# The last layer's modulation products move from the last block's attention into the recurrence, 24 of their steps behind its first inverse

## The chip, the cores and the metric

One core of one Trainium2 chip. The metric is the device time of one execution in microseconds (us), median of several runs. Profiles come from one profiled execution each; times inside it count from the start of its span. "Granted clock" is the share of full speed that TensorE's clock had; it has two levels, 1.2 GHz (0.50) and 2.4 GHz (1.00), and a stretch's figure is their mean.

## The reference, cut to what matters

Two stacked networks of two layers each act on 256 tokens of width 1024 (float32). Every layer is modulated: a condition vector, through SiLU, times a 1024 x 6144 matrix gives six rows (shift, scale, gate, twice).

```python
for l in range(2):                       # second network
    mod = (silu(c) @ ada_w[l] + ada_b[l])
    sh1, sc1, g1, sh2, sc2, g2 = split(mod, 6)
    h = rms_norm_2(x, norm1_g[l]) * (1 + sc1) + sh1
    y = even_mixer_2(h) if l % 2 == 0 else odd_mixer_2(h)   # attention
    x = x + g1 * y
    h = rms_norm_2(x, norm2_g[l]) * (1 + sc2) + sh2
    x = x + g2 * hier_moe(h)
```

The first network's second layer has a gated recurrence instead of attention. `wkv_scan` walks the tokens with S <- S*w - (S kk)(kk a)^T + v k^T in two directions, first over 256 context tokens, then over the 256 tokens of x, for 16 heads. The modulations depend on the condition vectors alone, so they can be computed at any time before they are used.

## The kernel before, in words

**Recurrence (`odd1`, L686).** The scan is computed in chunks of 64 tokens. The 16 heads are taken as two groups of eight, each first over the context, then over x: four passes, g = 0 to 3. A pass has four parts. `rw_feat` (L970) makes the features of a head pair (four calls per pass, each for two directions: small matmuls at L989, L1046 and L1056, many DVE and ACT operations, stores of `kb`, `ar` and `rb` to DRAM on ACT's DMA queue). `rw_inv` (L1085) inverts triangular blocks on DVE by 31 pairs of operations (L1101, L1102), each needing the one before. `rw_post` (L1105; `rw_post2` for g = 3) completes the inverses with 32x32 matmuls. `rw_chain` (L1165) takes the four chunks in order: a product with the inverse (L1220), state updates and output products (L172). Features of later passes are called inside earlier chains by `ahead(p)` and the table `pos`.

**Side work.** `ada_unit` (L191) is a generator for one 512-column piece of a modulation: a 1024 x 512 weight block against the condition, eight matmuls at L203 into one PSUM bank, of which four can run beside each other on four column groups of the array. The profile counts two MATMUL instructions for each, so 16 for a unit. Then come one ACT copy (L209), eight instructions at L213 (column form) or two at L217 (row form), and small DVE sinks (L255 or L271 and L273); a row unit also loads its bias and stores its result on GpSimd's queue (L264, L268, L275). The generator yields after each two matmuls: a step, of four MATMUL instructions. A unit has four steps. `tick(n, i)` (L227) draws n steps and ties each drawn matmul behind matmul i in TensorE's order, through `anchor`. `ada2(l)` (L1408) is all of the second network's layer l: 12 units, 48 steps.

In the recurrence a step loads its own 512 KB (`wn` = 2) on SP's queue into one of two buffers (`weights(2)`); the PSUM pool of the units has one buffer (`phase((3, 2, 1), 0)`). In the last block a step shares a 1 MB load with the next (`wn` = 4), out of ten buffers, and the PSUM pool has two buffers.

**Who draws.** `layer1` (L1288) sets the recurrence's side work: `gates(1, 0)`, `mods(1, 1)`, `gates(1, 1)`, `ada2(0)`, 80 steps. The table `tk` (L1284) says how many are drawn: one or two behind a feature matmul (four per head pair), and four behind each chunk's product at L1220, two for g = 2. The places offer 120; the 80 run out with the features that pass 1 calls for pass 2. `layerB(0)` (L1992) sets `ada2(1)`; its 48 steps are drawn in `causal_scores` (L1455): 24 in `even2` (L1489, layer 0's attention), 24 in `odd2` (L1562, layer 1's).

**Order.** The tile framework fixes each engine's order at build time, with program order as the priority and a timeline of its own for when operands are ready. On the chip each engine and each DMA queue goes through its list in that order. After the recurrence the two side buffers' place goes to the two tiles of x, reloaded on GpSimd's queue at L887 and needed by the residual at L385.

Of the kernel before, what the change touches and what calls it, by code (L numbers as in the profile page):

```python
# [110 lines left out]
class K:  # L111
# [55 lines left out]
    def chain(self):  # L167

        prev = [None]

        def mm(*a, **k):
            i = self.nc.tensor.matmul(*a, **k)  # L172
            if prev[0] is not None:
                self.after(i, prev[0])
            prev[0] = i
            return i
        return mm
# [486 lines left out]
class L1(K):  # L664
# [21 lines left out]
    def odd1(self, xs, cst, Acol, Bcol):  # L686
# [131 lines left out]
        with self.phase((3, 2, 1), 0) as ph:  # L818
            self.pl = ph.es.enter_context(tc.tile_pool(name="pl", bufs=1, space=PSUM, reuse_waits="tile"))
            gp = ph.pool("gp")  # L820
            St = [self.T(gp, [P, 2, 4, P], f"St{c}") for c in range(2)]
            E3 = [self.T(gp, [P, 4, 65], f"E3{d}") for d in range(2)]
            for c in range(2):
                nc.gpsimd.memset(St[c], 0.0)
                nc.gpsimd.memset(E3[c][:, :, 64 * c:64 * c + 1], 1.0)
            E = dict(E3=E3, kT=kTd, kkn=kknd, rT=rTd, St=St, twl=twl, tal=tal, hpar=hpar, hka=hka, vd=vd,
                     ms=mstrict, mi=mincl, rmask=rmask, yd=yd, Y1=Y1, bon=bon, rkI=rkI, kbd=[self.tc.dram_tile([2, 4, P, 4, P], F32, name=f"kb_dram{g}") for g in range(4)],
                     ard=[self.tc.dram_tile([2, 4, P, 4, P], F32, name=f"ar_dram{g}") for g in range(2)],
                     rbd=[self.tc.dram_tile([2, 4, P, 8, 64], F32, name=f"rb_dram{g}") for g in range(2)])
            st = None  # L830
            self.nq = 4
            F = self.rw_open(0, False, gp)
            for hp in range(4):
                self.rw_feat(hp, gp, E, F)
            for g in range(4):
                N = {"hp": 0}

                def ahead(p):

                    while g < 3 and N["hp"] < 4 and self.pos[g][N["hp"]] <= p:  # L840
                        if N["hp"] == 0:
                            N["F"] = self.rw_open((g + 1) // 2, g % 2 == 0, gp)
                        self.rw_feat(N["hp"], gp, E, N["F"])
                        N["hp"] += 1
                ahead(0)
                self.rw_inv(gp, F)
                ahead(1)
                rest = (self.rw_post2 if g >= self.g2 else self.rw_post)(gp, F)
                st = self.rw_chain(gp, E, F, st, ahead, rest)
                ahead(9)  # L850
                F = N.get("F")
                if F:
                    Fl = F
            F = Fl

            self.do(self.side)
            E.update(z=z, J=J, sgl=sgl, behind=F["inv"])
            sl = slice(512, 1024)
            nc.gpsimd.dma_start(lng1, A["lng"][sl].partition_broadcast(P))
            nc.gpsimd.dma_start(g21, A["g2"][:, sl])  # L860
            t2 = lambda n: self.T(gp, [P, 512], n, bufs=3 if n in ("BK", "ARx") else 2)
            lng, lnb, g2 = (t2("BK") for _ in range(3))
            nc.gpsimd.dma_start(lng, A["lng"][0:512].partition_broadcast(P))
            nc.gpsimd.dma_start(lnb, A["lnb"][0:512].partition_broadcast(P))
            nc.gpsimd.dma_start(g2, A["g2"][:, 0:512])
            for t in range(2):
                rows = slice(t * P, (t + 1) * P)
                y, y1 = t2("KB"), t2("ARx")
                nc.scalar.dma_start(z[:, t, :], vd[0][rows, 0:512])
                nc.scalar.dma_start(y, yd[0][rows, :])  # L870
                nc.scalar.dma_start(y1, yd[1][rows, :])
                self.rw_bonus(0, t, E, z[:, t, :], lnb)
                self.rw_readout(t, E, y, y1, t2("RB"), lng, g2, z[:, t, :])
            lnb = t2("BK")
            nc.gpsimd.dma_start(lnb, A["lnb"][sl].partition_broadcast(P))
            for t in range(2):
                nc.scalar.dma_start(z1[:, t, :], vd[0][t * P:(t + 1) * P, sl])
                self.rw_bonus(1, t, E, z1[:, t, :], lnb)
# [402 lines left out]
    def q(self, n):  # L1281
        return getattr(self.nc, self.qs[n])

    tk = ((1, 0), (1, 0), (1, 0), (1, 0)), ((1, 2), (1, 2), (1, 2), (1, 2)), (4, 4, 2, 4)  # L1284
    late, g2 = 1, 3
    pos = ((3, 4, 9, 9), (9, 9, 9, 9), (4, 9, 9, 9), (5, 9, 9, 9))

    def layer1(self):  # L1288
        nc = self.nc
        xs, cst = self.xs[:2], self.xs[2:]  # L1290
        self.at, self.side = "unit", chain(self.gates(1, 0), self.mods(1, 1), self.gates(1, 1), self.ada2(0))
        self.odd1(xs, cst, *self.modc[1, 0])
        self.early2()
        with self.phase() as ph:
            self.ar = ph.pool("ar1")
            self.ws = ph.pool("ws3", 2)
            self.mlp(xs, 1, *self.modc[1, 1], [0, 0], 1)
# [94 lines left out]
class B2(L1):  # L1392
# [600 lines left out]
    def layerB(self, l):  # L1993
        nc, A = self.nc, self.A
        xs = self.xs[:2]
        with self.phase() as ph:
            self.ar = ph.pool(f"arB{l}")
            self.ws = ph.pool(f"wsB{l}", 2)
            Ac, Bc = self.bmods[l]
            if l == 0:  # L2000
                self.at, self.side = "unit", self.ada2(1)
            hT = self.norm_mod_T(xs, Ac, Bc, [0, 0], rs=self.rn)
            mix = (self.even2 if l == 0 else self.odd2)(hT, ph)
            if l:
                self.do(self.side)
            else:
                self.flush()
            G = self.T(self.ar, [P, D], "gates", bufs=1)
            self.row(G, f"bda{l}", 2, 0)
            logits = self.out2(mix, A["b_out"] if l == 0 else A["n_out"], xs, G, *self.router(l))  # L2010
        with self.phase(ns2=5) as ph:
            self.ar = ph.pool(f"arM{l}")
            hs = [self.T(self.ar, [P, 2, D], n, F32R) for n in ("mo_hh", "mo_hl")]
            xd = [self.T(self.ar, [P, KT, 256], "mo_xd", bufs=2) for _ in range(1)]
            hb = [self.T(self.ar, [P, D], f"mo_h{t}") for t in range(2)]
            rows = []
            for b in (4, 3, 5):
                rows.append(self.T(self.ar, [P, D], f"mo_row{b}"))
                self.row(rows[-1], f"bda{l}", b, 0)
            if l:  # L2020
                fg = self.T(self.ar, [P, D], "mo_fin")
                nc.gpsimd.dma_start(fg, A["fin_g"].partition_broadcast(P))
                self.fin = fg, hb
            self.rn = self.moe(xs, l, logits, rows, hb, *hs)
            if l:
                for t in range(2):
                    if t:
                        nc.vector.tensor_scalar(hb[t], hb[t], self.rn[t], None, ALU.mult)
                    else:
                        nc.scalar.activation(hb[t], hb[t], AF.Copy, scale=self.rn[t])  # L2030
                    nc.sync.dma_start(self.out[t * P:(t + 1) * P, :], hb[t])
# [54 lines left out]
```

## Time and profile before

| | us |
|---|---|
| median of 3 runs (lowest, highest) | 2259.72 (2257.11, 2260.31) |
| profiled execution, its own time | 2250.88 |
| its span, first to last instruction | 2248.9 |
| mean granted clock | 0.936 |
| PE, DVE, ACT, POOL busy in the span | 2075.3, 1159.6, 856.6, 119.8 |

How to read it: a busy PE is not PE at its peak, since matmuls are pipelined and a slow clock makes them longer. What a piece of work costs is read from the stage in which it runs: which engine is full there, and which wait ends last. The recurrence stands at about 800 to 1291 us, its output projection until about 1330, the MLP until about 1500, layer 0's attention of the last network at about 1600 to 1670, layer 1's at about 1950 to 2060.

### The profile page before, as it was taken

The page shows a single profiled execution, that of the slowest core. Times are in us where ns is not written, and L with a number is a line of the kernel's source. Part 1 is how long each engine was busy: PE and PEld are TensorE (multiplying, and loading weights), DVE is VectorE, ACT ScalarE, POOL GpSimd, SP SyncE. Part 2 cuts the span into 40 slices and gives each one's busy share as a digit, 9 for nine tenths or more (in the row PEclk, how much of TensorE's full clock was granted, in tenths as well). Part 3 has the DMA queues.
Part 4 walks back from the last instruction along what each step waited for, and adds up shares of the span by engine and source line. Part 5 has one row for each costly group of instructions (what it writes and reads, how often), then busy time and mean ns, then how long its engine had stood idle before and what let it go on. Part 6 is the DMA issues. An engine that isn't in the chain of part 4 may idle for free. (4 is left out here: it accounts for less than half of the span.)

```text
span 2248.9 us, 32827 instructions
## 1 busy us (share of the span) xinstructions
PE 2075.3 (92%) x13114; PEld 1451.2 (65%) x13114; DVE 1159.6 (52%) x2419; ACT 856.6 (38%) x1650; POOL 119.8 (5%) x216
## 2 busy tenths in 40 slices
PE   7999899999989989899997789998998989999897
PEld 4864688888866675685652569987765439646542
DVE  2247543433465536866826265666664236475433
ACT  3334443322352446564432345544452114243211
POOL 0100000000021000001111100000000000010000
PEclk9999999999999998759897889999998999999898
DMA  7448212222332426736886555537464959452494
GB/s 285 142 186 322 76 73 94 94 94 94 113 128 89 140 100 211 228 92 200 263 280 192 177 217 183 187 118 272 171 252 163 386 202 354 156 206 96 179 383 173
DMA packets 124310, 414.53 MB, mean 184 GB/s; under 512 B 20608, under 2 KB 59152, under 8 KB 88432
## 3 DMA queue, kind: packets, MB, share of 16 engines
q1 hardware_dynamic: 59824, 340.03, 41.1%
q10 hardware_dynamic: 55552, 50.95, 7.3%
q0 software_dynamic: 8768, 21.31, 3.1%
q8 instruction: 107, 1.75, 0.3%
q14 instruction: 59, 0.48, 0.1%
HBM read 383.30 MB, written 28.93 MB: 183 GB/s over the span
## 5 line engine op out<-in xcount | busy, mean ns | idle before, releaser
L164 DVE TENSOR_TENSOR wlo<-wraw,whi 128x1024 fp32r<-128x1024 f32 x252 | 308.0, 1225 | 405.6 <-ACT whi L161 398.3
L161 ACT ACTIVATE whi<-wraw 128x1024 fp32r<-128x1024 f32 x252 | 265.4, 1058 | 490.2 <-PE mm L189 234.6
L187 PE MATMUL mm<-hT_h,whi 128*128 128x256 f32 (+1 forms) x832 | 268.2, 333 | 2.3 <-ACT whi L161 2.3
L188 PE MATMUL mm<-hT_l,whi 128*128 128x256 f32 (+1 forms) x832 | 267.3, 328 | 0.0
L189 PE MATMUL mm<-hT_h,wlo 128*128 128x256 f32 (+1 forms) x832 | 242.2, 327 | 0.5 <-DVE wlo L164 0.3
L203 PE MATMUL ada<-wraw,csil 128*32 128x512 f32 x768 | 148.1, 663 | 30.7 <-DMA wraw<-in_bda 19.7
L187 PEld LDWEIGHTS mm<-hT_h,whi 128*128 128x128 f32 x832 | 157.4, 191 | 19.8 <-ACT whi L161 4.0
L188 PEld LDWEIGHTS mm<-hT_l,whi 128*128 128x128 f32 x832 | 158.6, 191 | 14.9
L189 PEld LDWEIGHTS mm<-hT_h,wlo 128*128 128x128 f32 x832 | 149.2, 190 | 16.3 <-DVE wlo L164 1.5
L188 PE MATMUL mm<-wlo,b 128*128 128x512 f32 x384 | 151.3, 394 | 0.1
L189 PE MATMUL mm<-whi,b 128*128 128x512 f32 x384 | 150.8, 393 | 0.0
L1934 PE MATMUL ada<-wraw,mo_xd 128*64 128x512 f32 x512 | 135.5, 599 | 0.0
L187 PE MATMUL mm<-whi,b 128*128 128x512 f32 x384 | 135.1, 393 | 0.0
L310 PE MATMUL tr<-s,x 128*128 128x128 f32 x288 | 57.0, 342 | 50.4 <-DVE s L301 20.0
L188 PE MATMUL mm<-wlo,hT_h 128*128 128x512 f32 (+1 forms) x256 | 98.8, 388 | 1.4 <-DVE wlo L164 1.4
L189 PE MATMUL mm<-whi,hT_l 128*128 128x512 f32 (+1 forms) x256 | 95.9, 388 | 0.0
L187 PE MATMUL mm<-whi,hT_h 128*128 128x512 f32 (+1 forms) x256 | 95.3, 398 | 0.5 <-ACT whi L161 0.4
L310 PEld LDWEIGHTS tr<-s,x 128*128 128x128 f32 x288 | 48.9, 240 | 62.0 <-issue 33.7
L188 PEld LDWEIGHTS mm<-wlo,b 128*128 128x128 f32 x384 | 72.0, 188 | 17.9 <-DVE wlo L164 0.8
L187 PEld LDWEIGHTS mm<-whi,b 128*128 128x128 f32 x384 | 72.0, 188 | 16.6
L189 PEld LDWEIGHTS mm<-whi,b 128*128 128x128 f32 x384 | 72.0, 188 | 16.4
L1934 PEld LDWEIGHTS ada<-wraw,mo_xd 128*64 128x64 f32 x512 | 38.1, 136 | 67.9 <-issue 67.7
(520 smaller groups left out, 3714.6 us busy)
## 6 DMA issues: line engine op xcount, KB each, us to landing
wraw<-in_w SPq DMA_DIRECT2D x64, 1024.0 KB, 4.8
wraw<-in_moe_gu SPq DMA_DIRECT2D x64, 1024.0 KB, 7.8
wraw<-in_ada SPq DMA_DIRECT2D x32, 1024.0 KB, 7.2
wraw<-in_moe_d SPq DMA_DIRECT2D x32, 1024.0 KB, 7.1
wraw<-in_bda SPq DMA_DIRECT2D x48, 512.0 KB, 4.7
wraw<-in_bda SPq DMA_DIRECT2D x24, 1024.0 KB, 4.8
wraw<-in_ada SPq DMA_DIRECT2D x32, 512.0 KB, 4.8
wraw<-in_b_in SPq DMA_DIRECT2D x12, 1024.0 KB, 11.5
```

What stands on the lines that cost most here:

```text
L161: nc.scalar.activation(h, src, AF.Copy)
L164: nc.vector.tensor_tensor(l, src, h.bitcast(F32), ALU.subtract)
L187: mm(ps, ah, bh, start=first, stop=False)
L188: mm(ps, ah, bl, start=False, stop=False)
L189: mm(ps, al, bh, start=False, stop=last)
L203: i = nc.tensor.matmul(ps[q:q + 32, :], lhs[:, k, :], raw[:, j % self.wn, :], start=k < nq, stop=k >= 8 - nq, tile_position=(0, q))
L310: nc.tensor.matmul(pt[:, j, :], xs[e + j][:, k * P:(k + 1) * P], dall[:, e + j, :], start=True, stop=True)
L1934: nc.tensor.matmul(pg[64 * e:64 * e + 64, :], xd[:, k, s0:s0 + 64], gu[e](k), start=k == 0, stop=k == KT - 1, tile_position=(0, 64 * e))
```

## The change

After `rw_inv` of pass g, `ti[g]` steps are drawn without an anchor: 24 for g = 0, none for the others. Pass 2 draws four steps per chunk instead of two. `ada2(1)` is appended to the recurrence's side work, 128 steps in all, and `layerB` no longer sets or drains any; the calls of `tick` in `even2` and `odd2` stay, and draw nothing.

```diff
                 ahead(0)
                 self.rw_inv(gp, F)
+                self.tick(self.ti[g])
                 ahead(1)
...
-    tk = ((1, 0), (1, 0), (1, 0), (1, 0)), ((1, 2), (1, 2), (1, 2), (1, 2)), (4, 4, 2, 4)
+    tk = ((1, 0), (1, 0), (1, 0), (1, 0)), ((1, 2), (1, 2), (1, 2), (1, 2)), (4, 4, 4, 4)
+    ti = (24, 0, 0, 0)
...
-        self.at, self.side = "unit", chain(self.gates(1, 0), self.mods(1, 1), self.gates(1, 1), self.ada2(0))
+        self.at, self.side = "unit", chain(self.gates(1, 0), self.mods(1, 1), self.gates(1, 1), self.ada2(0), self.ada2(1))
...
-            if l == 0:
-                self.at, self.side = "unit", self.ada2(1)
             hT = self.norm_mod_T(xs, Ac, Bc, [0, 0], rs=self.rn)
             mix = (self.even2 if l == 0 else self.odd2)(hT, ph)
-            if l:
-                self.do(self.side)
-            else:
-                self.flush()
```

## Rows read from the trace of the kernel before

**Rows 1.** Stages in windows: busy us (instructions) of each engine, granted clock, DMA share.

```profile
core 0: us, PE busy (x) PEld busy (x) DVE busy (x) ACT busy (x) POOL busy (x), PEclk, DMA share, GB/s
917.00:1016.00 99.00, 93.47 (x638) 75.96 (x640) 77.26 (x215) 61.67 (x149) 1.11 (x2) 0.59 0.45 131
1016.00:1180.00 164.00, 151.03 (x2175) 94.33 (x2173) 93.70 (x234) 68.77 (x124) 22.72 (x43) 0.94 0.81 253
1180.00:1257.00 77.00, 58.58 (x744) 25.80 (x744) 48.57 (x104) 20.99 (x35) 10.86 (x21) 0.80 0.63 197
1257.00:1291.00 34.00, 24.32 (x440) 19.55 (x438) 4.23 (x9) 11.94 (x20) 3.18 (x7) 0.91 0.46 146
1291.00:1332.00 41.00, 30.29 (x113) 22.57 (x114) 30.34 (x46) 19.96 (x34) 0.00 (x0) 0.91 0.75 305
1603.00:1669.00 66.00, 63.64 (x402) 36.02 (x400) 42.17 (x151) 33.47 (x105) 2.60 (x5) 1.00 0.67 251
1960.00:2028.00 68.00, 64.56 (x391) 27.70 (x383) 51.38 (x188) 27.55 (x103) 7.89 (x14) 0.93 0.55 203
```

**Rows 2.** The same windows, line L203 alone: PE busy (x), PEld busy (x), clock, DMA.

```profile
845.00:917.00 72.00, 14.62 (x64) 2.00 (x64) 0.87 0.76 233
917.00:1016.00 99.00, 0.00 (x0) 0.00 (x0) 0.59 0.45 131
1016.00:1180.00 164.00, 45.41 (x176) 6.13 (x176) 0.94 0.81 253
1180.00:1257.00 77.00, 22.86 (x80) 2.83 (x80) 0.80 0.63 197
1603.00:1669.00 66.00, 13.83 (x96) 2.66 (x96) 1.00 0.67 251
1960.00:2028.00 68.00, 13.75 (x96) 2.72 (x88) 0.93 0.55 203
```

**Rows 3.** The same windows, lines L213 (first row) and L217 (the others) alone.

```profile
1603.00:1669.00 66.00, 4.21 (x32) 3.87 (x32) 1.00 0.67 251
1603.00:1669.00 66.00, 2.04 (x4) 0.17 (x4) 1.00 0.67 251
1960.00:2028.00 68.00, 6.24 (x12) 0.52 (x12) 0.93 0.55 203
```

**Rows 4.** PE's groups at L203: in 1016 to 1180, then in 1180 to 1257 (last column: idle before).

```profile
L203 PE MATMUL ada<-wraw,csil 128*32 128x512 f32 x176 | 45.4, 657 | 11.7 <-DMA wraw<-in_bda 3.6 <-DMA wraw<-in_ada 3.6 <-DVE bB L255 2.4
L203 PE MATMUL ada<-wraw,csil 128*32 128x512 f32 x80 | 22.9, 777 | 17.0 <-DMA wraw<-in_bda 16.1 <-DVE adb L271 1.0
```

**Rows 5.** PE and DVE in time order: start, us, what [idle before and releaser].

```profile
1187.14 1.05 PE L203 MATMUL ada<-wraw,csil 128*32 128x512 f32 x4 [3.45 <-DMA wraw<-in_bda]
...
1193.85 1.06 PE L203 MATMUL ada<-wraw,csil 128*32 128x512 f32 x8
...
1254.27 1.92 PE L203 MATMUL ada<-wraw,csil 128*32 128x512 f32 x4 [0.68 <-DMA wraw<-in_bda]
...
1328.33 1.27 DVE L385 SCALAR_TENSOR_TENSOR x<-yo,ss,x 128x1024 f32<-128x1024 f32 x1
```

**Rows 6.** GpSimd's queue in time order, and two DMA issues of 1180 to 1257.

```profile
1256.50 1.06 POOL L887 DMA_DIRECT2D x<-x_dram  x2 [9.24 <-DMA UV<-v_dram]
...
wraw<-in_bda SPq DMA_DIRECT2D x18, 512.0 KB, 4.5
...
x<-x_dram POOLq DMA_DIRECT2D x1, 512.0 KB, 5.8
```

**Rows 7.** Waits of 907 to 985; even2's attention as a window; DVE's L271 in 1960 to 2028.

```profile
DVE AB L1074 <- PE tr L1056: 6.4, 5, 1.6
DVE AB L1069 <- PE tr L1056: 3.2, 4, 1.6
...
1618.00:1653.00 35.00, 35.00 (x246) 18.97 (x245) 27.55 (x115) 18.33 (x64) 0.00 (x0) 1.00 0.64 243
...
L271 DVE TENSOR_TENSOR adb<-ada,adb 2x512 f32<-2x512 f32 x6 | 4.0, 675 | 1.1 <-PE ada L217 1.1
```

## The prediction

> **What bounds the kernel now.** I read the stages as windows first, then the same windows for L203 alone, then the orders of PE and of GpSimd's queue at the ends of stages. The side work has three surroundings. In 917 to 1016, the first inverses, there is none of it: L203 counts zero, PE is busy 93.5 of 99 us, but at a granted clock of 0.59, with DVE at 77.3 [rows 1, 2]. From 1016 to 1256 it runs without a break, at a pace of its own: 176 instructions, four to a step, make 44 steps in 164 us, 3.73 us each, then 20 steps in 77 us, 3.85 each [rows 2]. The anchors aren't the limit: the last steps drawn hang on pass 2's features and run in the middle of pass 3's chain. The limit is the load of 512 KB through two buffers. It lands in 4.5 us [rows 6]; in 1180 to 1257 PE stood idle 16.1 us before L203 for it, in the 164 us before only 7.2 [rows 4]. From 1257 to 1291 there is no side work. In the last block the 48 steps sit in stages in which PE is full: 63.6 of 66 us in layer 0's attention, 64.6 of 68 in layer 1's [rows 1], with no wait for weights there.
>
> So the change takes PE time out of two full stages, puts half of it beside a cold stretch, and hangs the other half onto a queue that is already late. The sign is decided by when the last side step ends.
>
> **What is moved.** 48 steps are 192 instructions at L203, 12 copies at L209, 32 instructions at L213 (four units), 16 at L217 (eight), the sinks on DVE; on SP 24 loads of 1 MB go and 48 of 512 KB come; on GpSimd's queue ten loads and eight stores of rows move to the recurrence.
>
> **Last block, gain.** Side work there takes 13.8 + 4.2 + 2.0 = 20.0 us of PE in the first window and 13.8 + 6.2 = 20.0 in the second [rows 2, 3]. Instructions overlap a little in these sums, so 37 us is the upper bound. What is late next is DVE: it keeps 42.2 us in the first, less two L271 at 0.675, so 40.8, and 51.4 - 4.0 = 47.4 in the second [rows 1, 7]. It doesn't fill a stage of softmaxes that wait in turn for PE and ACT: its share in the attention part was 27.55 of 35.00, 0.79 [rows 7]. At that share the stages take 40.8 / 0.787 = 52 and 47.4 / 0.787 = 60 us, 14 and 8 less. I take **-22**; the lower bound is -8, if only the less crowded half of it comes back. The 24 loads that leave SP's queue there give nothing: PE's groups in these windows show no wait for weights.
>
> **The 24 steps behind the first inverses.** Without an anchor, and ahead of almost everything else by program order, they can run as their loads land: at 3.73 us a step 24 take 90 us, within the 99 that are empty of side work. They are two units of columns left of `mods(1, 1)`, `gates(1, 1)`, and two of `ada2(0)`. PE: 24 x 45.41 / 44 = 24.8 us, and six units' ends, four at 4.21 / 4 and two at 2.04 / 2, 6.2; together 31 [rows 2, 3]. If PE stays at 0.59 there is no room: 31 us measured near 0.94 become 49, and 93.5 + 49 = 143 against 99, a loss of 44. If the clock is what it was in 1016 to 1180 with side work, 0.94, the old work shrinks to 93.5 x 0.59 / 0.94 = 59; with 31, and 7.2 / 44 = 0.16 us of waiting per step, that is 94 us. The best that can come is DVE's 77, so -22. I take 0.94, since 1016 to 1180 is the nearest stretch that mixes small matmuls with these steps: **-5** for the start of pass 0's chain. Behind a waiting L203 stand L1056 and L989 of the features and L1122 of `rw_post` on PE, and DVE waits for these already (9.6 us at L1069 and L1074 [rows 7]); that is why a gain above 5 isn't taken.
>
> The rule of the Trainium skill on this (TensorE: Matmul & The Clock Gate, section "What's actually happening") is that the throttled clock is the default and activity releases it. By a full release the old work would take 93.5 x 0.59 = 55 us, with 35 of new 90, and the term would be -9 in place of -5.
>
> **The 24 steps at the end.** The other 24 are drawn in pass 2 and come last in the queue. Up to there order and lag are as before, with the gained 5 us: the side work stands at about 1256.2 - 5 = 1251 (the last step starts at 1254.27 and takes 1.92 [rows 5]) with 24 steps to go. For the pace I take the end of the old work, 18 steps with starts from 1193.85 to 1254.27, so 60.4 / 17 = 3.55 us [rows 5]: 24 x 3.55 = 85, and the last step ends at 1336. The lower bound is two loads in flight and nothing else in the way, (4.5 + 1.05) / 2 = 2.8 us, end at 1318; the upper bound is above 3.85, for loads that share the DMA engines with the output projection's weights (DMA share 0.75 in 1291 to 1332 [rows 1]).
>
> Who waits for that: pass 3's chain, whose products queue behind waiting steps (as 3.45 us at 1187 did [rows 5]); PE has 34 - 24.3 and 41 - 30.3, so 20 us, idle from 1257 to 1332 for 24.8 + 8 x 1.02 = 33 us of new PE work, which takes some 13 us more than there is. Later than that is x: its two tiles lie where the side buffers lay, and its loads were issued at 1256.50, right at the end of the last step, after 9.24 us of waiting [rows 6]. The profile names a DMA as releaser; the time fits the step. They land 5.8 us later. At 1336 this gives 1342, and L385, which needs x, stood at 1328.33 [rows 5]. So the recurrence ends **+14** later, the 5 us already in it; the 13 of PE work lie beside that. KB loads of the chain and the rows' small transfers share GpSimd's queue; I cost them at nothing beside the 14, and at up to 10 where x's loads are laid ahead of a chain's load.
>
> **Sum.** -22 + 14 = -8 us: the profiled execution's 2250.9 becomes 2243. The median is 8.8 us above that execution, and the same difference on it gives 2252.
>
> **Rivals.**
>
> (a) *The side work outlasts the projection; slower.* With -22 in the last block the point at which it decides is an end of the last step at 1336 + 8 = 1344, a pace of 93 / 24 = 3.9 us. That is hardly above the 3.85 of 1180 to 1257, and the new loads also meet four loads of 1 MB for the projection, on the same SP queue. At 4.4 us the end is 1251 + 106 = 1357, x comes at 1363, 35 late, and the sum is +13: 2273. For it: the 16.1 us of waits [rows 4]. Against it: after 1291 neither chain nor features compete. Chance 0.26.
>
> The Trainium skill (DMA: Bandwidth & Descriptors, section "Queues, rings and completion order") says that a DMA engine takes turns between the queues it has work for, packet by packet. By that rule the side loads and the projection's slow each other, and it speaks for (a); no row here shows the two together.
>
> (b) *The attention cools; no change.* Without the dense steps PE may not keep 1.00 there. The first inverses show small matmuls alone at 0.59 [rows 1]. At 0.70 layer 0's stage needs (63.6 - 20) / 0.70 = 62 us on PE, 4 less than now, and layer 1's (64.6 - 20) x 0.93 / 0.70 = 59, 9 less: -13 + 14 = +1, 2261. Against it: projections run beside both stages. Chance 0.18.
>
> (c) *The cold stretch stays cold*, or the 24 steps aren't laid there: +44 in place of -5, 2301. Against it: 0.94 and 0.87 wherever features and L203 ran together [rows 2]. Chance 0.06.
>
> (d) *Both ends good*: pace 2.8, so that x isn't late, and -30 in the last block: some 2230. Chance 0.08.
>
> **How the numbers follow.** The forecast has 0.42. A measurement of this kernel tells 0.2%, 4.5 us, from no change. Faster by more: forecast and (d), 0.50; within: (b), 0.18; slower: (a) and (c), 0.32. The range leaves out (c), half of (d) and the far end of (a): 2229 to 2284. The forecast's own spread, with the pace from 3.4 to 3.85 and the last block from -17 to -30, is 2240 to 2264.
>
> **What would show it.** Right: about 96 instructions of L203 between 917 and 1016 and a granted clock near 0.9 there; pass 0's first product at L1220 some 5 us earlier; L203 until about 1336; x loaded right behind its last step and L385 some 14 us late; the two attention stages at about 52 and 60 us, still at 0.9 or more. Wrong: L385 more than 22 us late, attention stages that shrink by less than 14 us together, or a first stretch longer than 99 us.

## The result and the profile after

The change makes the kernel slower: 2332.77 us median of four runs (2325.98 to 2337.05) against 2259.94 (2257.11 to 2260.31), a ratio of 1.0322 (95% interval 1.0295 to 1.0349). The forecast was 2252 with a range of 2229 to 2284; the result lies outside. The profiled execution of the changed kernel took 2325.98 us, its span is 2324.2 us, its mean granted clock 0.920. Medians are taken over undisturbed executions; one of e7's four, 2411.82 us at a clock of 0.891, is left out as slow.

Cutting both traces at the same instructions shows where the 75 us of span went (us; starts of the instructions named):

| from, to | before | after | difference |
|---|---|---|---|
| span's start, first inverse | 907.8 | 903.4 | -4.4 |
| first inverse, last chain product (L1220, now L1221) | 378.0 | 377.6 | -0.4 |
| last chain product, residual L385 | 42.5 | 120.8 | +78.3 |
| L385, first scores of layer 0's attention | 275.4 | 275.3 | -0.1 |
| first to last scores there | 48.1 | 35.2 | -12.9 |
| last scores, first scores of layer 1's attention | 295.6 | 296.8 | +1.2 |
| first scores there, first product of its MoE | 154.7 | 170.0 | +15.3 |
| first product of its MoE, end | 146.6 | 145.1 | -1.5 |

One place carries the loss, the 121 us behind the last chain product. The two attention stages, which were to give back 22 us, give back nothing together.

The stages as windows of the changed kernel (line numbers are one or two higher from L847 on), in the order of [rows 1]: busy us (instructions) of PE, PEld, DVE, ACT, POOL, granted clock, DMA share, GB/s. Then layer 0's attention (1677 to 1712) and layer 1's.

```profile
917.00:1016.00 99.00, 89.31 (x704) 56.94 (x705) 69.00 (x190) 56.17 (x133) 4.14 (x8) 0.83 0.75 234
1016.00:1180.00 164.00, 147.18 (x2083) 87.22 (x2078) 111.65 (x281) 72.42 (x136) 25.83 (x48) 0.94 0.81 256
1180.00:1257.00 77.00, 66.22 (x988) 39.39 (x984) 37.53 (x76) 25.03 (x42) 6.46 (x12) 0.85 0.60 192
1291.00:1332.00 41.00, 16.48 (x36) 1.66 (x36) 6.66 (x7) 5.20 (x6) 2.50 (x5) 0.52 0.89 353
...
1677.00:1692.00 15.00, 14.42 (x85) 10.01 (x83) 11.18 (x32) 10.64 (x25) 0.00 (x0) 1.00 0.47 151
1692.00:1712.00 20.00, 19.41 (x107) 10.80 (x107) 17.27 (x82) 10.61 (x45) 0.00 (x0) 1.00 0.11 45
...
2027.00:2047.00 20.00, 19.31 (x71) 9.94 (x73) 13.00 (x49) 5.95 (x26) 0.00 (x0) 0.50 0.00 0
2047.00:2067.00 20.00, 20.00 (x76) 9.53 (x73) 9.86 (x37) 5.26 (x23) 0.00 (x0) 0.50 0.01 1
2067.00:2096.00 29.00, 25.90 (x108) 12.12 (x108) 15.38 (x58) 7.97 (x34) 0.00 (x0) 0.62 0.00 1
```

Three things are to be seen. In 1291 to 1332, where the output projection ran before with 113 matmuls, PE now has 36, DVE 7 instructions, and DMA is at 0.89. Layer 0's attention is shorter at a full clock. In layer 1's, PE is busy nearly without a break and yet at 0.50, and DMA does nothing.

Line L203 alone in 917 to 1016, 1016 to 1180, 1180 to 1257 and behind the last chain product (PE, PEld, clock, DMA, GB/s); [rows 2] answer to it:

```profile
917.00:1016.00 99.00, 24.47 (x93) 3.15 (x92) 0.83 0.75 234
1016.00:1180.00 164.00, 42.81 (x168) 5.86 (x168) 0.94 0.81 256
1180.00:1257.00 77.00, 19.84 (x84) 2.52 (x80) 0.85 0.60 192
1281.00:1364.00 83.00, 30.43 (x80) 3.64 (x80) 0.59 0.71 258
```

The first stretch took its 24 steps (93 instructions). But 80 instructions, 20 steps, still stand behind the last chain product, in 83 us. PE in order of time there:

```profile
1281.03 1.15 PE L1221 MATMUL mm<-rhs,AB 64*64 64x64 f32 x32 [0.43 <-ACT rhs L1215]
...
1300.81 3.43 PE L203 MATMUL ada<-wraw,csil 128*32 128x512 f32 x8 [4.92 <-DMA wraw<-in_bda]
1318.53 3.19 PE L203 MATMUL ada<-wraw,csil 128*32 128x512 f32 x8 [14.29 <-DMA wraw<-in_bda]
...
1359.28 1.74 PE L203 MATMUL ada<-wraw,csil 128*32 128x512 f32 x4 [0.58 <-DMA wraw<-in_bda]
1361.78 1.02 PE L217 MATMUL ada<-adp,sel 128*2 128x512 f32 x2 [0.76 <-ACT adp L209]
1362.73 0.66 PE L899 MATMUL tr<-ident,z 128*128 128x128 f32 x4
...
1364.07 0.50 PE L187 MATMUL mm<-whi,moh 128*128 128x512 f32 x1
```

From 1287 to 1362 PE has nothing but side steps, most of them after a wait for their load; L899, which prepares the projection's operand, follows without a gap behind the last, and the projection's first product 1.3 us later. So the projection waits for no data of its own: it stands in PE's list behind the steps (e5 tests it). The load of x on GpSimd's queue and the residual, which ends the stage:

```profile
1361.33 1.06 POOL L888 DMA_DIRECT2D x<-x_dram  x2 [7.56 <-PE ada L203]
...
1401.86 1.27 DVE L385 SCALAR_TENSOR_TENSOR x<-yo,ss,x 128x1024 f32<-128x1024 f32 x1
```

The longest wait, 14.3 us, is explained by SP's queue, and by its loads of 1286 to 1320 (KB each, median us from issue to landing):

```profile
1286.06 1.61 SPq L151 DMA_DIRECT2D wraw<-in_wo  x3
1287.97 5.73 SPq L151 DMA_DIRECT2D wraw<-in_bda  x2
1293.74 0.42 SPq L151 DMA_DIRECT2D wraw<-in_wo  x1
1294.46 5.32 SPq L151 DMA_DIRECT2D wraw<-in_w  x5
1302.76 1.84 SPq L151 DMA_DIRECT2D wraw<-in_bda  x2
```

```profile
wraw<-in_w SPq DMA_DIRECT2D x6, 1024.0 KB, 15.8
wraw<-in_wo SPq DMA_DIRECT2D x4, 1024.0 KB, 10.5
wraw<-in_bda SPq DMA_DIRECT2D x4, 512.0 KB, 14.1
```

`in_w` are the MLP's weights. Five blocks of 1 MB that nobody needs before the projection is done were issued just ahead of two side loads of 512 KB. The four side loads issued in this stretch, two behind the projection's blocks (`in_wo`) and two behind the MLP's, landed after 14.1 us (median) in place of 4.5 [rows 6].

### The profile page after: what moved, and what is told of

It is laid out like the page before. It is cut to its first block, busy times and chain, and to the rows that moved or that the text cites. A ratio compares the mean times of both kernels' runs of the same rounds, so it can differ in the third digit from the quotient of the medians.

```text
span 2324.2 us, 32897 instructions
## 1 busy us (share of the span) xinstructions
PE 2106.3 (91%) x13114; PEld 1442.3 (62%) x13114; DVE 1161.5 (50%) x2419; ACT 857.6 (37%) x1650; POOL 119.8 (5%) x216
## 5 line engine op out<-in xcount | busy, mean ns | idle before, releaser
L164 DVE TENSOR_TENSOR wlo<-wraw,whi 128x1024 fp32r<-128x1024 f32 x252 | 307.5, 1223 | 419.6 <-ACT whi L161 412.9
L161 ACT ACTIVATE whi<-wraw 128x1024 fp32r<-128x1024 f32 x252 | 266.0, 1060 | 509.8 <-PE mm L189 237.6
L203 PE MATMUL ada<-wraw,csil 128*32 128x512 f32 x768 | 175.8, 687 | 64.2 <-DMA wraw<-in_bda 52.3
L203 PEld LDWEIGHTS ada<-wraw,csil 128*32 128x32 f32 x768 | 25.3, 114 | 124.8 <-DMA wraw<-in_bda 72.7
L209 ACT ACTIVATE adp<-ada 128x512 f32<-128x512 f32 x48 | 28.5, 594 | 151.2 <-PE ada L203 148.7
L187 PEld LDWEIGHTS mm<-whi,b 128*128 128x128 f32 x384 | 72.0, 188 | 16.6
```

Of the source, the lines that this page charges most:

```text
L161: nc.scalar.activation(h, src, AF.Copy)
L164: nc.vector.tensor_tensor(l, src, h.bitcast(F32), ALU.subtract)
L187: mm(ps, ah, bh, start=first, stop=False)
L203: i = nc.tensor.matmul(ps[q:q + 32, :], lhs[:, k, :], raw[:, j % self.wn, :], start=k < nq, stop=k >= 8 - nq, tile_position=(0, q))
L209: nc.scalar.activation(part[kr], ps[kr], AF.Copy)
```

## The experiments

Theory: the last side steps lag behind their places, the loads set their pace, and the projection stands behind all of them in PE's list; layer 0's attention gains, layer 1's loses its clock. The rivals stand with each run. `ada2a(l)` yields the first 24 steps of `ada2(l)` (the columns and row 2), `ada2b(l)` the other 24 (rows 3, 4, 5). Medians in us, each beside runs of the kernel before on the same chip; that kernel's median differs by up to 10 us between chips, so totals from different chips are compared as differences from it. The ratio is estimated from the runs of both and isn't the quotient of the two medians:

| kernel | median | before | ratio (95%) |
|---|---|---|---|
| changed kernel | 2332.77 | 2259.94 | 1.0322 (1.0295 to 1.0349) |
| e1_cold_only | 2233.78 | 2258.14 | 0.9889 (0.9847 to 0.9931) |
| e2_half | 2240.72 | 2258.14 | 0.9914 (0.9886 to 0.9941) |
| e3_warm | 2306.12 | 2258.14 | 1.0196 (1.0141 to 1.0252) |
| e5_behind | 2271.63 | 2257.88 | 1.0048 (1.0017 to 1.0079) |
| e6_four_buffers | 2316.37 | 2257.88 | 1.0243 (1.0168 to 1.0318) |
| e7_no_cold | 2384.82 | 2257.88 | 1.0538 (1.0455 to 1.0620) |
| e8_router | 2234.38 | 2257.88 | 0.9900 (0.9840 to 0.9960) |
| e9_56_steps | 2213.76 | 2249.62 | 0.9827 (0.9796 to 0.9858) |
| e10_24_behind | 2220.99 | 2249.62 | 0.9892 (0.9834 to 0.9950) |
| e11_odd_late | 2297.07 | 2249.62 | 1.0201 (1.0161 to 1.0242) |
| e12_48_behind | 2248.69 | 2257.08 | 0.9966 (0.9941 to 0.9991) |

Lengths of stages in each trace (us). A trace is one execution, and its own time lies between 17 us below its kernel's median (e5) and 10 above it (e9). A first inverse to pass 0's first product at L1221; B to the last chain product; C to L385; D from there to the MLP's residual; E first to last scores of layer 0; F first scores of layer 1 to its MoE.

| kernel | A | B | C | D | E | F |
|---|---|---|---|---|---|---|
| before | 92.1 | 285.9 | 42.5 | 192.7 | 48.1 | 154.7 |
| changed kernel | 91.2 | 286.5 | 120.8 | 192.7 | 35.2 | 170.0 |
| e1 | 94.0 | 262.2 | 44.0 | 192.7 | 48.1 | 155.9 |
| e2 | 90.2 | 283.0 | 42.4 | 191.9 | 35.2 | 157.0 |
| e3 | 93.4 | 282.0 | 120.3 | 192.7 | 35.2 | 152.4 |
| e4 | 88.5 | 278.8 | 79.3 | 192.7 | 35.2 | 149.7 |
| e5 | 89.0 | 274.0 | 46.3 | 204.1 | 35.2 | 170.3 |
| e6 | 87.5 | 282.2 | 105.9 | 192.0 | 47.4 | 155.6 |
| e7 | 93.4 | 296.2 | 166.4 | 192.7 | 35.2 | 171.6 |
| e8 | 88.7 | 262.2 | 42.6 | 192.4 | 42.4 | 155.4 |
| e9 | 88.3 | 251.5 | 43.6 | 200.0 | 48.1 | 153.1 |
| e10 | 87.5 | 262.3 | 42.6 | 198.3 | 35.2 | 154.0 |
| e11 | 93.4 | 282.6 | 43.4 | 192.7 | 48.1 | 205.4 |
| e12 | 88.1 | 244.9 | 46.3 | 238.3 | 35.2 | 156.5 |

**One part alone: the 24 unanchored steps.**

```diff
 (the kernel before)
+                self.tick(self.ti[g])        # behind rw_inv
+    ti = (24, 0, 0, 0)
```

> The kernel before with 24 of its 80 recurrence steps drawn behind the first inverses; the last layer's 48 steps stay in the last block. Theory: the only effect is the first product of pass 0, 5 us earlier, since the same stretch of the changed kernel gained 5 us: about 2255 us (2250 to 2259), no change in the last block. Rival: the 80 steps now run out some 90 us earlier, near 1170, and what comes after them in passes 2 and 3 is cooler than the granted clock of 0.80 that 1180 to 1257 had, or shows no gain: 2260 to 2275.

2233.78 us, 24 less, outside both ranges. Column A did not shrink (94.0), but B did, by 24 us: the side work runs out at 1189, and passes 2 and 3 go on without it. The clock is near what [rows 1] had there, 0.81 in 1180 to 1270. So the steps that the kernel before ran in passes 2 and 3 were in the chain's way, at about 1 us a step, and what the 24 places behind the inverses bring is that fewer stand there. On which engine or queue they were in the way isn't separated.

**Half of the move.** On top of e1:

```diff
-        ... self.gates(1, 1), self.ada2(0))
+        ... self.gates(1, 1), self.ada2(0), self.ada2a(1))
-            if l == 0:                       # layerB
-                self.at, self.side = "unit", self.ada2(1)
+            if l:
+                self.at, self.side = "unit", self.ada2b(1)
```

> 104 steps in the recurrence (24 behind the first inverses, the first 24 of the last layer at the end of the queue, pass 2 at two per chunk as before), the other 24 steps in layer 1's attention as before, none in layer 0's. Theory: the 104th step started at 1270 in the changed kernel, before its last chain product, so the projection isn't held up: -5 at the first inverses, -13 in layer 0's attention, layer 1's attention at a granted clock of 1.00 as before: about 2242 us (2234 to 2250). Rival: the end of the recurrence is held up by these 24 steps too, by 10 to 20 us: 2252 to 2262.

2240.72: the theory holds. C is 42.4, as before: 104 steps end in time. E is 35.2, F 157.0. The 5 us that the theory put at the first inverses came as 1.9 in A and 2.9 in B, so there it was right by its sum only. Against e1 the 24 steps in passes 2 and 3 cost B 21 us and bring E 13.

**Matmuls put back into layer 1's attention.** The changed kernel (cut; called behind the scores, 8 times, with n = 3, so 48 matmuls, which the profile counts as 96):

```diff
+        for k in range(2 * n):
+            q = 32 * (k % 4)
+            i = self.nc.tensor.matmul(ps[q:q + 32, :], self.cs2[:, k % KT, :], ...
```

> The changed kernel with matmuls of the same size as the 24 side steps put back into layer 1's attention, on operands that already lie in SBUF, into a bank that nobody reads: no load, no copy, no sink. Theory (clock): the granted clock of that stage, 0.50 to 0.62 for 80 us, comes back to 0.9 or more, and the stage is as long as it was in the kernel before: 2333 - 16 = 2317 us (2312 to 2323), although PE has some 16 us more to do. Rival (it was the loads, or the order of the work, and not the matmuls): the matmuls only add, 2333 to 2350, with a clock below 0.7.

F fell to 152.4 with more work in it, and the clock is back:

```profile
2036.00:2056.00 20.00, 18.72 (x114) 8.58 (x114) 14.30 (x56) 7.61 (x33) 0.00 (x0) 1.00 0.00 1
2056.00:2076.00 20.00, 19.77 (x127) 8.50 (x129) 12.94 (x50) 6.00 (x26) 0.00 (x0) 1.00 0.01 1
2076.00:2101.00 25.00, 22.95 (x135) 11.11 (x131) 15.95 (x60) 8.68 (x38) 0.00 (x0) 0.93 0.00 1
```

DMA is as idle as in the changed kernel, so it is the matmuls, not their loads. Each against its own before, the total gained 25 us (72.8 to 48.0), F in the two traces 17.6. The median lies 6 us below the theory's range; where these came from isn't shown.

**The same from the other side.** The kernel before, without the draws in `odd2`:

```diff
-        self.tick(steps, i)
+        if steps < 3:
+            self.tick(steps, i)
```

> The kernel before, with the 24 steps of layer 1's attention drawn behind that attention and not in it. Theory (these steps keep the clock of that stage): the granted clock falls to 0.5 to 0.65 between the first scores and the output projection, the stage from the first scores to the MoE's first product grows from 155 to 170 us or more, and the total to 2258 + 15 = 2273 us, and up to 15 more where the 24 steps aren't hidden by the output projection (2270 to 2290). Rival (they only fill PE, and the attention is shorter without them): 2245 to 2262, with a clock above 0.8.

2297.07, 47 above its own before where the theory had 12 to 32, so beyond its range on its side: F is 205.4. The attention ran at 0.50 from 1965 to 2060, and the 24 steps came on top:

```profile
1965.00:1985.00 20.00, 19.03 (x67) 9.82 (x65) 14.51 (x57) 6.75 (x30) 0.00 (x0) 0.50 0.00 0
1985.00:2005.00 20.00, 18.60 (x71) 9.04 (x71) 8.39 (x31) 4.69 (x19) 0.00 (x0) 0.50 0.00 1
```

**Last steps without loads.** The changed kernel (cut); rows 3 to 5 of the last layer are computed from a tile that lies in SBUF:

```diff
-                if j % self.wn == 0:
+                if self.res is None and j % self.wn == 0:
...
-  raw[:, j % self.wn, :]
+  raw[:, j % self.wn, :] if self.res is None else self.res
```

> The changed kernel, whose last 24 side steps read a tile that already lies in SBUF in place of their weight blocks, so that 12 MB of loads in the recurrence are left out and three rows of the last layer's modulation are not what they should be; every matmul, copy, sink and small transfer stays. Theory (the loads set the pace of the last steps, and the output projection stands behind them on PE): the last step ends before 1290 and the residual's first half stands near 1325 to 1335 in place of 1402: about 2262 us (2255 to 2275). Rival (the units' own chain through one PSUM bank, or the work on PE, holds them up): the last step ends after 1330, 2300 us or more.

The total says nothing here: the wrong rows feed the router, and layer 1's MoE ran its first products with 1024 matmuls in place of 256. In the recurrence the last step started at 1313.9, 46 us earlier, and L385 at 1357.3, 44.6 earlier. So loads are the larger part of the lateness, and the projection moves with the last step; but the theory's 1290 was missed (the last step ended at 1315, short of the rival's 1330). What held the steps up next, in PE's order:

```profile
1287.44 1.02 PE L217 MATMUL ada<-adp,sel 128*2 128x512 f32 x2 [0.78 <-ACT adp L209]
1303.18 3.34 PE L203 MATMUL ada<-rwc,csil 128*32 128x512 f32 x16 [14.73 <-DVE adb L271]
```

and on ACT and DVE:

```profile
1299.09 2.00 ACT L161 ACTIVATE whi<-wraw 128x1024 fp32r<-128x1024 f32 x2 [9.82 <-DMA wraw<-in_w]
...
1300.18 2.36 DVE L164 TENSOR_TENSOR wlo<-wraw,whi 128x1024 fp32r<-128x1024 f32 x2 [9.46 <-ACT whi L161]
1302.46 0.67 DVE L271 TENSOR_TENSOR adb<-ada,adb 2x512 f32<-2x512 f32 x1
```

The row's sink L271 stands in DVE's list behind a split of the weights (L161 and L164), which waits for one of the MLP's blocks of 1 MB. The units have one PSUM bank, and the next step waits for the sink.

**Last steps behind the projection.** The changed kernel:

```diff
-        ... self.ada2(0), self.ada2(1))
+        ... self.ada2(0), self.ada2a(1))
                     half(j, u, ps[u][j])
+            self.do(self.ada2b(1))
```

> The changed kernel, whose last 24 side steps (three rows of the last layer) are drawn behind the recurrence's output projection in program order, not ahead of its end. Theory (the projection stands behind these steps in PE's order): the residual's first half comes some 80 us earlier than 1402, near 1325; the 24 steps then take their 25 us of PE, and 6 for their units' ends, ahead of or inside the MLP, which has no PE to spare: 2333 - 78 + 30 = 2285 us (2275 to 2296). Rival (the loads are the cost wherever they stand): 2310 us or more.

2271.63, 3 us below the theory's range: C is 46.3, so the 24 steps had held the projection up for 75 us. Behind it they cost D 11 us for 31 of PE work, less than the theory took; here they share loads of 1 MB in eight buffers, and wait for none of them. PE of this kernel:

```profile
1269.93 1.15 PE L1222 MATMUL mm<-rhs,AB 64*64 64x64 f32 x32 [0.75 <-ACT rhs L1216]
...
1276.02 2.07 PE L940 MATMUL tr<-y,rwc 128*128 128x512 f32 x2 [2.49 <-DVE mol L903]
...
1279.92 1.03 PE L187 MATMUL mm<-whi,moh 128*128 128x512 f32 x2
```

The projection starts 10 us after the last chain product (L1222 in this kernel), against 83.

**Fewer early loads.** The changed kernel with `self.weights(4)` in place of `self.weights(8)` behind the recurrence.

> The changed kernel with four weight buffers of 1 MB in place of eight behind the recurrence, so that the projection's four loads fill them and the MLP's six early loads of 1 MB can't share the DMA engines with the last side steps (they had held the first step after 1301 up by 14 us). Theory (contention): the last side step starts near 1346 in place of 1360, the residual near 1388, and the total gains what the MLP doesn't lose by its later loads: 2318 to 2333 us. Rival (the steps are as late without these loads): last step at 1355 or later, total 2330 to 2345.

The last step started at 1344.3 and L385 at 1386.6, as the theory said; C is 15 us shorter, D stayed at 192.0, and the total is 14 us less, each against its own before (2316.37 is 2 below the theory's range). PE's idle time before L203 behind the last chain product, in 1281 to 1364, fell from 33.6 to 24.8 us for `in_bda` (changed kernel, then this one):

```profile
L203 PE MATMUL ada<-wraw,csil 128*32 128x512 f32 x80 | 30.4, 974 | 35.9 <-DMA wraw<-in_bda 33.6 <-DVE adb L271 2.3
L203 PE MATMUL ada<-wraw,csil 128*32 128x512 f32 x80 | 27.1, 812 | 27.4 <-DMA wraw<-in_bda 24.8 <-DVE adb L271 2.4
```

So the MLP's early loads cost some 15 us. This run also shows layer 0's attention long and layer 1's short, with no steps in either; see the end.

**The cold places undone.** The changed kernel with `ti = (0, 0, 0, 0)`.

> The changed kernel without the 24 steps behind the first inverses: all 128 steps are tied to matmuls, the last of them in pass 3's chain. Theory (the 24 steps behind the first inverses cost nothing there, and each step at the end costs about 3.5 us, since loads set the pace and the projection stands behind them): 24 x 3.5 = 84 us more: 2333 + 84 = 2417 us (2395 to 2430). Rival (the loads behind the inverses only put off other traffic, and the side work catches up before the end): 2330 to 2360.

2384.82: 54 more than the changed kernel, each against its own before, where 84 were expected. In the trace B grew by 10, C by 46: the last step starts at 1421.9, 62 us later, so a step at the end costs 2.6 us, not 3.5. The side work catches up a little, by its pace once nothing else runs: 38 steps in 127 us are 3.3 each. The value lies between theory and rival, nearer to the theory.

**Places of a lower price.** e8 moves 16 steps behind layer 0's router logits (e1 with this and the matching order of units, cut):

```diff
+            if l == 0:                       # moe, behind logits(i)
+                self.do(self.side)
```

> 80 steps in the recurrence, 24 of them behind the first inverses; of the last layer's 48 steps 8 stay in layer 0's attention, 16 move behind that layer's router logits, where PE was idle for 6 of 22 us at a granted clock of 0.69, and 24 stay in layer 1's attention. Theory (a step costs by the room that its stage has): layer 0's attention gives back 16 x 0.54 = 9 us, the router takes some of it: 2234 - 5 = 2229 us (2220 to 2236). Rival (the steps stand ahead of the router's own small matmuls on PE, which nothing hides): 2240 to 2255.

2234.38, in the upper part of the theory's range, and no gain on e1. E gave back 5.7, not 9, and the way from the last scores to the MoE's first product took it: 61 us in e1, 73 here. The rival's mechanism holds, at a smaller price than it named.

e9 and e10 move 24 steps each behind the projection, e12 both:

```diff
 (e1)
-        ... self.gates(1, 1), self.ada2(0))
+        ... self.gates(1, 1), self.ada2a(0))
                     half(j, u, ps[u][j])
+            self.do(self.ada2b(0))           # e9
+            self.do(self.ada2a(1))           # e10: ada2(0) whole as in e1, layerB as in e2
```

> 80 steps for the recurrence became 56: 24 behind the first inverses, 32 in all the rest, and the last 24 (three rows of the last network's layer 0) run behind the output projection, where 24 steps had made the MLP 11 us longer. The last layer's 48 steps stay in the last block as before. Theory (24 steps fewer in passes 2 and 3 had shortened the recurrence by some 20 us; the next 24 do the same in passes 1 and 2): 2234 - 20 + 11 = 2225 us (2216 to 2232). Rival (only what ran beside passes 2 and 3 was in the way, and the clock falls where features run alone): 2234 + 11 = 2245 us or more.

2213.76. The kernel before was itself 8 us quicker on this chip; against it that is 36 less, inside the 26 to 42 that the theory's range gave. Against e1, B fell by another 10.7, half of what the theory had, D rose by 7.3, and A fell by 5.7, though its steps are those of e1: that is scatter between executions. This is the best kernel of the study, 1.7% below the kernel before.

> 80 steps in the recurrence, 24 of them behind the first inverses; the first 24 steps of the last layer run behind the recurrence's output projection in place of layer 0's attention, the other 24 stay in layer 1's attention. Theory (prices measured so far): 2234 + 11 behind the projection - 13 in layer 0's attention = 2232 us (2225 to 2240). Rival (with these steps there the MLP starts later by all of their 31 us on PE): 2245 to 2255.

2220.99, 29 less than its own before, inside the theory's 18 to 33: E is 35.2 and D 198.3, so 13 us are won for 6.

> Both moves together: 56 steps in the recurrence, 24 of them behind the first inverses; 48 steps (three rows of layer 0, the first 24 of the last layer) behind the output projection, none in layer 0's attention, 24 in layer 1's as before. Theory (the room behind the projection is used up by the first 24, which cost 7 us there; from then on PE is full at a granted clock of 1.00 and the next 24 cost their 31 us): 2214 - 13 + 31 = 2232 us (2222 to 2238). Rival (the second 24 cost as little as the first): 2214 - 13 + 7 = 2208 us (2200 to 2215).

2248.69, worse than both: D is 238.3, 46 for 48 steps. The theory had PE full at a clock of 1.00 there. But in 1300 to 1340 PE runs side steps alone, at 0.72, and is idle for 11.8 us; in 1250 to 1420, 8.7 us of its idle time before L203 end with a row's sink:

```profile
1300.00:1340.00 40.00, 28.17 (x161) 10.01 (x154) 4.89 (x12) 6.07 (x9) 4.74 (x10) 0.72 0.83 305
...
L203 PE MATMUL ada<-wraw,csil 128*32 128x512 f32 x192 | 32.9, 743 | 8.7 <-DVE adb L271 8.7
```

## Why the prediction was wrong, step by step

- **What bounds it now.** That the loads set the pace of the side work was right (e4, e6). What the steps of passes 2 and 3 cost the chain was put at nothing without a reason, though [rows 5] show 3.45 us of it once; e1 shows 24 us in all. In the changed kernel this moved nothing, since about as many stand there as before (B 286.5, before 285.9).
- **The 24 steps behind the first inverses, -5.** Right as to the place and the clock's rise, to 0.83 in place of 0.94; the size isn't borne out. A went from 92.1 to 91.2. Pass 0's first product did come 5.4 us earlier, but 4.4 of these were there at the first inverse already, a point that scatters from 903.4 to 917.2 in the traces: luck. Over the eleven traces that have the steps A is 89.7 on average (87.5 to 94.0), over the three that haven't (before, e7, e11) 93.0. The full release of which the Trainium skill speaks (TensorE: Matmul & The Clock Gate, "What's actually happening") was to give -9; the clock did rise from 0.59 with the added work, but no trace shows the 9.
- **The 24 steps at the end, +14: the step that failed.** The prediction named x as what waits longest ("Later than that is x") and put PE's work "beside" the steps. Measured is +73.5 at L385 (1328.3 to 1401.9), 60 beyond the term, in two parts. The last step ended at 1361, not 1336 (+25): the point with 24 steps to go, taken at 1251, came at 1270, since the 41st step started at 1016, where the 17th had before, so that no lead was there, and the next 64 took 3.97 us each, before 3.75; the last 24 took 91 us for 85, with the MLP's loads in the way (e6). And behind the last step came not 6 us for x but 41, the whole output projection (+35). x was indeed loaded from 1361.3 on, behind the last step, but it was there long before the projection's end. PE went through its matmuls in the order of its list, and the list has the steps first (e5: with them behind it, the projection starts 10 us after the last chain product). The Trainium skill says the same (TensorE: Matmul & The Clock Gate, "Step-by-step: what each phase is for": matmuls stay in program order), and the trace agrees, with no gap between 1361.78 and 1362.73. The prediction knew the rule of the lists, but applied it to the chain's products only.
- **Last block, -22.** Layer 0's part, -14, was right in size: 48.1 to 35.2 (e2, e10 too). Its reason, that DVE is late next at a share of 0.79, isn't shown: DVE's share is 0.81, but PE is still busy 33.8 of 35 us. Layer 1's -8 was wrong by its sign, +15.3: rival (b), the attention that cools, at 0.50 rather than its 0.70, in one of the two stages (e3, e11).
- **Rival (a)**, at +13, had the place and one half of the mechanism, the steps that outlast the chain and meet larger loads on SP's queue; its last step, at 1357, is 4 us from the measured one. It fell short since it too let only x wait. The Trainium skill's rule beside it (DMA: Bandwidth & Descriptors, "Queues, rings and completion order"), engines that take turns between queues, isn't what happened here, and doesn't speak for (a), since both kinds of load were on SP's queue: that queue carried 12.96 of the 13.49 MB of 1286 to 1320, and the side loads stood in line behind their own queue's blocks. Rival (c), nearer by its 2301, had the wrong place: the first stretch did not get longer.
- **The range.** It ended at 2284 because in every case at the recurrence's end only x waited. With the projection behind the steps the prediction's own 1336 + 41 would have put L385 at 1377, 49 late, and the forecast on the slower side.

## What to carry over

Work that fills gaps has a price for each place, and it is read best from a trace of that stage without it. 24 steps with 31 us of PE work (the prediction's estimate) cost here: nothing that stands out of the scatter behind the first inverses, 13 in layer 0's attention, 6 to 11 behind the projection (46 for 48), 11 to 24 in passes 1 to 3, some 75 ahead of the projection, and in layer 1's attention they were worth 15 where the clock fell without them. Before moving such work, write down for the last piece what stands behind it in each engine's list, not only what reads its result, and which larger loads its queue has ahead of it.

## What the runs showed of the hardware that was not expected

A stage in which PE is busy all the time can run at either clock level. Layer 1's attention without side steps or matmuls in their place had 19.3 to 20.0 of 20 us busy at 0.50 in the changed kernel. With them F is 152.4 to 157.0 in eight traces, the one of before among them; without, it was 170.0, 170.3 and 171.6, but also 149.7 (e4) and 155.6 (e6), where the clock came back within the stage. Layer 0's attention without steps had E at 35.2 in eight traces, and 47.4 in e6, where the clock fell (first line; the second is layer 1's, same kernel):

```profile
1692.00:1710.00 18.00, 18.00 (x57) 9.11 (x56) 8.39 (x36) 5.21 (x20) 0.00 (x0) 0.50 0.00 1
...
2051.00:2071.00 20.00, 17.39 (x111) 9.00 (x110) 15.21 (x59) 7.92 (x34) 0.00 (x0) 1.00 0.00 1
```

With the 24 steps, or the matmuls of e3, the stage was short in all eight traces. What tips a run without them was not settled.
